# A scan of log-sum-exp on one core: an opening store of one element per DMA engine, the last waits moved inside the block, and the last tile leaving by 1, 1 and 2 rows

## The chip, the cores and the metric

One core of a Trainium2 chip runs the kernel. The metric is device time in microseconds (us), the median of several executions. Executions of one kernel mostly agree within 0.3 us of 1250. "PE" is the matrix engine, "DVE" the vector engine, "ACT" the scalar engine (it also issues the stores), "POOL" or GpSimd the general engine (it makes two masks and has little else to do), "SP" the sync engine (it issues the loads).

## The reference, cut to what matters

```python
x: (8, 4096, 2048) float32
out[:, 0] = x[:, 0]
for t in range(1, 4096):
    out[:, t] = logaddexp(out[:, t - 1], x[:, t])     # written out with max, exp and log
```

That is a running log of a sum of exponentials along the second axis: exp, a running sum, then log. 268 MB come in and 268 MB go out.

## The kernel before

The 4096 rows of each batch are cut into tiles of 512 rows (128 partitions with 4 rows each, 2048 columns). There are 64 tiles of 4 MB and six buffers of 32 KB per partition. For each tile ACT takes exp; DVE adds the 4 rows of each partition (L186); PE adds the sums of the partitions before (L166) and the carry of the tile before (L155); DVE adds both in (L195); ACT takes Ln (L130) and issues the store (L135). SP issues a load as soon as the store of the buffer's last content has landed (L110).

```python
for rows, c in ((slice(0, 2), top), (slice(2, R), loaded[0])):        # L84, before the block
    c(nc.sync.dma_start(out=ti[0][:, rows, :], in_=x_v[0][:, rows, :]), 16)
with nc.Block() as block:
    ...
    # SP
    for n in range(1, NT):
        i = n % NI
        if n >= NI:
            sp.wait_ge(stored[i].s, n // NI * 16)
        loaded[i](sp.dma_start(out=ti[i][:], in_=x_v[n]), 16)
    ...
    # ACT, tile n, half h of the columns; parts(n) is the whole tile, two halves for the last one
    for rows in parts(n) if h else [slice(0, R)]:
        logs(act.activation(t[:, rows, half[h]], t[:, rows, half[h]], ACT.Ln)._wait_ge(carried[h].s, n + 1))
        if h:
            act.wait_ge(logs.s, logs.n)
            stored[n % NI](act.dma_start(out=o_v[n][:, rows, :], in_=t[:, rows, :]), 16)
    # ACT's order: exp(0); for n: exp(n + 1), ln(n)
    ...
for c in stored:                                                       # after the block
    nc.sync.wait_ge(c.s, c.n)
```

The softmax here doesn't subtract the row's maximum and nothing guards it: scores larger than these inputs give would overflow.

## Time and profile before

| | before |
|---|---|
| time, median of the three executions known when the prediction was made | 1250.37 us (1250.36 to 1250.6) |
| span of the profiled execution | 1248.8 us |
| first load packet | 2.04 us |
| first store issued / its first packet | 38.93 / 43.55 us |
| last load lands / last store lands | 1207.88 / 1246.77 us |
| last landing to span's end | 2.06 us |

Times inside an execution are from the span's start. A *semaphore* is a counter that instructions and transfers of the kernel raise and on which its engines wait; a transfer has *landed* with the last step that it adds there. Two readings beyond the page's lines are used throughout. A *packet record* is the start and duration of one piece of a transfer on one of the 16 DMA engines (a 32 KB packet normally takes 1.213 us, a 16 KB one 0.611 us: the medians in before, where 16038 of the 16128 packets of 32 KB took under 1.23 us). *Excess* is what packets took beyond that, summed over a stretch and divided by the 16 engines: the time that each engine lost. The profile's lines of before are in the prediction below.

### The profile page before, as it was taken

The numbers are of one execution on the slowest core, as the hardware profiler recorded it, in microseconds if no ns is written. First come the engines' busy times: TensorE is split into PE (matmuls) and PEld (weight loads), VectorE is DVE, ScalarE is ACT, GpSimd is POOL, SyncE is SP. The second block draws the span as 40 slices with busy tenths as digits, with TensorE's granted clock in tenths as the row PEclk, the third lists the DMA queues.
The fourth block names the chain that finished last, engine by engine and source line by source line (L and its number), as shares of the span: only waits on it lengthen the run. The fifth ranks groups of instructions, "written<-read, shape, count | busy, mean of one in ns | idle before, by whom it ended". The sixth has DMA issues, their size and how long they took to land.

```text
span 1248.8 us, 2916 instructions
## 1 busy us (share of the span) xinstructions
PE 645.1 (52%) x960; PEld 213.4 (17%) x960; DVE 1022.3 (82%) x512; ACT 907.5 (73%) x259; POOL 1.1 (0%) x8
## 2 busy tenths in 40 slices
PE   2655456553556444655465544555545564455551
PEld 0211112111112111211111111111111121111110
DVE  5999978778787787887878878778787787877873
ACT  5987866867768677686776866867768677686773
POOL 0000000000000000000000000000000000000000
PEclk9899788787887868777678786787767878778776
DMA  9999999999999999999999999999999999999998
GB/s 403 420 431 431 430 437 436 427 434 432 437 435 426 435 432 437 433 428 435 431 437 433 430 435 430 437 431 432 436 430 436 432 432 435 431 436 432 431 435 361
DMA packets 18735, 537.06 MB, mean 430 GB/s; under 512 B 2080, under 2 KB 2080, under 8 KB 2080
## 3 DMA queue, kind: packets, MB, share of 16 engines
q1 hardware_dynamic: 9360, 268.44, 49.9%
q10 hardware_dynamic: 9360, 268.44, 49.8%
q8 instruction: 7, 0.11, 0.0%
q14 instruction: 8, 0.07, 0.0%
HBM read 268.44 MB, written 268.44 MB: 430 GB/s over the span
## 4 chain that ended last, share of the span: by engine, by line
DMA 80%; ACT 14%; DVE 4%; PE 1%; DVEq 0%; issue 0%; SPq 0%; ACTq 0%; PEldq 0%
DMA out_dram<-ti 41%; DMA ti<-in_x_dram 38%; ACT ti L130 7%; ACT ti L121 7%; DVE ti L195 2%; DVE ti L186 1%; PE ps L166 1%; DVEq L86 0%; PE ps L155 0%; SPq L84 0%; ACTq L135 0%; PEldq L151 0%; SPq L233 0%; SPq L69 0%
## 5 line engine op out<-in xcount | busy, mean ns | idle before, releaser
L121 ACT ACTIVATE ti<-ti 128x4096 f32<-128x4096 f32 (+1 forms) x128 | 452.5, 3582 | 308.2 <-DMA ti<-in_x_dram 306.0
L186 DVE TENSOR_TENSOR ti<-ti 128x1024 f32<-128x1024 f32 x384 | 464.6, 1224 | 196.6 <-ACT ti L121 187.9
L195 DVE TENSOR_TENSOR ti<-ti,ps 128x4096 f32<-128x4096 f32 x128 | 560.0, 4416 | 9.0 <-PE ps L166 8.8
L166 PE MATMUL ps<-ti,before 128*128 128x512 f32 x512 | 373.2, 879 | 347.1 <-DVE ti L186 347.0
L130 ACT ACTIVATE ti<-ti 128x4096 f32<-128x4096 f32 x129 | 455.8, 3576 | 9.5 <-PE ps L155 6.6
L155 PE MATMUL ps<-ti,last 128*128 128x512 f32 x448 | 271.9, 738 | 228.9 <-DVE ti L195 228.9
L166 PEld LDWEIGHTS ps<-ti,before 128*128 128x128 f32 x512 | 127.5, 276 | 607.4 <-DVE ti L186 503.2
L155 PEld LDWEIGHTS ps<-ti,last 128*128 128x128 f32 x448 | 85.9, 212 | 399.5 <-DVE ti L195 332.8
L119 ACT ACTIVATE ti<-ti 128x4096 f32<-128x4096 f32 x1 | 3.6, 3616 | 6.3 <-DMA ti<-in_x_dram 6.3
L30 ACT ACT_TABLE_LOAD x1 | 1.3, 1283 | 0.8 <-PEq L222 0.8
L94 POOL TENSOR_SCALAR_AFFINE_SELECT before<-before 128x128 f32<-128x128 f32 x1 | 0.3, 292 | 0.1
L99 POOL TENSOR_SCALAR_AFFINE_SELECT last<-last 128x128 f32<-128x128 f32 x1 | 0.3, 292 | 0.0
L90 POOL MEMSET before<- 128x128 f32 x1 | 0.2, 204 | 0.5 <-SPq L69 0.5
L91 POOL MEMSET last<- 128x128 f32 x1 | 0.2, 204 | 0.0
L222 POOL MEMSET const-bfloat16-1.0<- 128x1 bf16 x1 | 0.1, 101 | 0.0
L222 POOL MEMSET const-uint8-127<- 128x1 uint8 x1 | 0.1, 101 | 0.0
L222 POOL MEMSET const-float32-0.0<- 128x1 f32 x1 | 0.1, 98 | 0.3 <-issue 0.3
L222 POOL MEMSET const-float32-1.0<- 128x1 f32 x1 | 0.1, 98 | 0.0
## 6 DMA issues: line engine op xcount, KB each, us to landing
ti<-in_x_dram SPq DMA_DIRECT2D x63, 4096.0 KB, 38.5
out_dram<-ti ACTq DMA_DIRECT2D x63, 4096.0 KB, 44.0
ti<-in_x_dram SPq DMA_DIRECT2D x2, 2048.0 KB, 9.6
out_dram<-ti ACTq DMA_DIRECT2D x2, 2048.0 KB, 13.2
```

Source lines behind the costliest of these rows:

```text
L30: nc.scalar.preload_act_table_set("natural_log_exp_and_others")
L90: ones(g.memset(before[:], 1.0))
L94: shaped(g.affine_select(out=before[:], in_=before[:], compare_op=mybir.AluOpType.is_ge, fill=0.0, base=-1, pattern=[[1, P]], channel_mult ...
L99: shaped(g.affine_select(out=last[:], in_=last[:], compare_op=mybir.AluOpType.is_ge, fill=0.0, base=-(P - 1), pattern=[[0, P]], channel_mu ...
L119: act.activation(t[:, :lo], t[:, :lo], ACT.Exp)._wait_ge(top.s, 16)
L121: a = act.activation(t[:, lo:, half[h]], t[:, lo:, half[h]], ACT.Exp)
L130: logs(act.activation(t[:, rows, half[h]], t[:, rows, half[h]], ACT.Ln)._wait_ge(carried[h].s, n + 1))
L155: m = pe.matmul(ps[(n + 1) % 2][:, sl], last[:], ti[n % NI][:, R - 1, sl], start=True, stop=False, skip_group_check=True,)
L166: m = pe.matmul(ps[n % 2][:, sl], before[:], ti[n % NI][:, R - 1, sl], start=n % NBLK == 0, stop=True, skip_group_check=True,)
L186: a = dve.tensor_add(t[:, r, cols], t[:, r - 1, cols], t[:, r, cols])
L195: joined[h](dve.tensor_add(t[:, :, cols], t[:, :, cols], ps[n % 2][:, cols].unsqueeze(1).to_broadcast([P, R, HALF]),)._wait_ge(ahead[h].s, ...
L222: nc = _bacc.Bacc("TRN2", target_bir_lowering=False, num_devices=1)
```

## The change

Its intent: pay at the start, where nothing flows, what the prediction takes for the cost of the store queue's first use (0.89 us of each DMA engine at 40 us); have fewer instructions after the last store has landed; give the last rows to the DMA engines sooner. The core of the diff, cut:

```diff
-        m = 2 if n == NT - 1 else 1
-        return [slice(k * R // m, (k + 1) * R // m) for k in range(m)]
+        return [slice(0, 1), slice(1, 2), slice(2, R)] if n == NT - 1 else [slice(0, R)]
...
-            self.s, self.n = tc.alloc_semaphore(name), 0
+            self.s, self.n = nc.alloc_semaphore(name), 0
...
+        def settle(self, engine):     # one instruction: wait until the count is n, then subtract n
...
-    with tc.tile_critical():
+    with tc.tile_critical(no_gpsimd_drain=True):
...
-        with nc.Block() as block:
+        with nc.Block(no_gpsimd_drain=True) as block:
             @block.scalar
             def _(act):
+                with nc.allow_non_contiguous_dma(reason="one element per DMA engine"):
+                    warm(act.dma_start(
+                        out=o_v[0][0:16, 0, 0:1], in_=nc.const_aps.tensor(0.0, [16, 1], f32)
+                    ), 16)
...
                 exp(0)
+                warm.now(act)         # wait for the opening store
...
+            @block.sync               # the first two loads move in here
...
+                for n in range(NT - NI, NT):
+                    stored[n % NI].settle(sp)
...
+            @block.gpsimd             # at its end, once ACT, PE and DVE have said they are over
+                over.now(g)
+                for c in every:
+                    if c not in stored:
+                        c.settle(g)
-        for c in stored:
-            nc.sync.wait_ge(c.s, c.n)
```

More of the change, by code (lines that the diff above doesn't have):

```diff
@@ L53, in parts @@
     def parts(n):
-        m = 2 if n == NT - 1 else 1
-        return [slice(k * R // m, (k + 1) * R // m) for k in range(m)]
+        return [slice(0, 1), slice(1, 2), slice(2, R)] if n == NT - 1 else [slice(0, R)]
+    every = []
     class Count:
         def __init__(self, name):
-            self.s, self.n = tc.alloc_semaphore(name), 0
+            self.s, self.n = nc.alloc_semaphore(name), 0
+            every.append(self)
         def __call__(self, inst, by=1):
@@ L66, in __call__, with add, now @@
             self.n += by
-            return self.n
-    with tc.tile_critical():
+        def add(self, engine):
+            engine.sem_inc(self.s, 1)
+            self.n += 1
+        def now(self, engine):
+            engine.wait_ge(self.s, self.n)
+        def settle(self, engine):
+            if self.n:
+                engine.add_instruction(mybir.InstEventSemaphore(
+                    name=f"I-{nc.next_id()}", engine=engine.engine, ins=[], outs=[],
+                    sync_info=mybir.SyncInfo(
+                        on_wait=[mybir.SyncWait(
+                            sync_type="semaphore", id=self.s.num, ant_name=self.s.name,
+                            wait_mode="sem-ge-imm", wait_value=self.n,
+                        )],
+                        on_update=[mybir.SyncUpdate(
+                            sync_type="semaphore", id=self.s.num, ant_name=self.s.name,
+                            update_mode="sem-sub-imm", update_value=self.n,
+                        )],
+                    ),
+                ))
+    with tc.tile_critical(no_gpsimd_drain=True):
         def counts(name, n):
             return [Count(f"{name}{i}") for i in range(n)]
-        ones, shaped, logs, top, chain = (
-            Count(s) for s in ("ones", "shaped", "logs", "top", "chain")
+        ones, shaped, logs, top, chain, warm, over = (
+            Count(s) for s in ("ones", "shaped", "logs", "top", "chain", "warm", "over")
         )
@@ L80 @@
         )
-        for rows, c in ((slice(0, 2), top), (slice(2, R), loaded[0])):
-            c(nc.sync.dma_start(out=ti[0][:, rows, :], in_=x_v[0][:, rows, :]), 16)
-        with nc.Block() as block:
-            @block.gpsimd
-            def _(g):
-                ones(g.memset(before[:], 1.0))
-                ones(g.memset(last[:], 1.0))
-                g.wait_ge(ones.s, ones.n)
-                shaped(g.affine_select(
-                    out=before[:], in_=before[:], compare_op=mybir.AluOpType.is_ge, fill=0.0,
-                    base=-1, pattern=[[1, P]], channel_multiplier=-1,
-                ))
-                shaped(g.affine_select(
-                    out=last[:], in_=last[:], compare_op=mybir.AluOpType.is_ge, fill=0.0,
-                    base=-(P - 1), pattern=[[0, P]], channel_multiplier=1,
-                ))
-            @block.sync
-            def _(sp):
-                for n in range(1, NT):
-                    i = n % NI
-                    if n >= NI:
-                        sp.wait_ge(stored[i].s, n // NI * 16)
-                    loaded[i](sp.dma_start(out=ti[i][:], in_=x_v[n]), 16)
+        with nc.Block(no_gpsimd_drain=True) as block:
             @block.scalar
             def _(act):
+                with nc.allow_non_contiguous_dma(reason="one element per DMA engine"):
+                    warm(act.dma_start(
+                        out=o_v[0][0:16, 0, 0:1], in_=nc.const_aps.tensor(0.0, [16, 1], f32)
+                    ), 16)
                 def exp(n):
@@ L133, in ln @@
                             if h:
-                                act.wait_ge(logs.s, logs.n)
+                                logs.now(act)
                                 stored[n % NI](act.dma_start(
@@ L143, in _ @@
                     ln(n)
+                over.add(act)
+            @block.sync
+            def _(sp):
+                for rows, c in ((slice(0, 2), top), (slice(2, R), loaded[0])):
+                    c(sp.dma_start(out=ti[0][:, rows, :], in_=x_v[0][:, rows, :]), 16)
+                for n in range(1, NT):
+                    i = n % NI
+                    if n >= NI:
+                        sp.wait_ge(stored[i].s, n // NI * 16)
+                    loaded[i](sp.dma_start(out=ti[i][:], in_=x_v[n]), 16)
+                for n in range(NT - NI, NT):
+                    stored[n % NI].settle(sp)
             @block.tensor
@@ L150, in carry @@
                         pe.wait_ge(joined[h].s, n + 1)
-                        pe.sem_inc(carried[h].s, 1)
+                        carried[h].add(pe)
                         return
@@ L172, in triangle @@
                     ahead[h](m)
-                pe.wait_ge(shaped.s, shaped.n)
+                pe.wait_ge(shaped.s, 2)
                 for n in range(NT):
@@ L179, in _ @@
                         carry(n, h)
+                over.add(pe)
             @block.vector
@@ L204, in _ @@
                         join(n, h)
-        for c in stored:
-            nc.sync.wait_ge(c.s, c.n)
+                over.add(dve)
+            @block.gpsimd
+            def _(g):
+                ones(g.memset(before[:], 1.0))
+                ones(g.memset(last[:], 1.0))
+                ones.now(g)
+                shaped(g.affine_select(
+                    out=before[:], in_=before[:], compare_op=mybir.AluOpType.is_ge, fill=0.0,
+                    base=-1, pattern=[[1, P]], channel_multiplier=-1,
+                ))
+                shaped(g.affine_select(
+                    out=last[:], in_=last[:], compare_op=mybir.AluOpType.is_ge, fill=0.0,
+                    base=-(P - 1), pattern=[[0, P]], channel_multiplier=1,
+                ))
+                over.now(g)
+                for c in every:
+                    if c not in stored:
+                        c.settle(g)
 _INS = ['x']
```

## The prediction

Its sum came to -0.7 + 0.1 + 0.0 = -0.6 us on 1250.37, so 1249.8, and 1249.7 with the lean. The 0.2 us at the head, which is in the -0.7, is an estimate: that the first issues of ACT and SP hold each other up was not shown. The "fetches" are the transfers that the page of before lists as q8 and q14, kind "instruction": 7 of 16 KB and 8 of 8 KB. "1.213 us everywhere else" is the normal time: 27 other 32 KB packets of before took 1.30 us or more, 14 of them started within 1 us after a fetch did. "No such excess" at later stores is at most 0.09 us in the 7 us after an issue.

> **What bounds the kernel now.** I read the page's slices first, then its queues, the stretches, the sync engine's waits and the timeline of the two ends.
>
> The slices (40 equal slices of the span; the digit is the busy share in tenths) and the queues:
>
> ```profile
> span 1248.8 us, 2916 instructions
> DMA  9999999999999999999999999999999999999998
> ...
> q1 hardware_dynamic: 9360, 268.44, 49.9%
> q10 hardware_dynamic: 9360, 268.44, 49.8%
> ```
>
> The transfers are busy in every slice; loads (q1) and stores (q10) share the 16 DMA engines almost evenly. 536.9 MB must move whatever the change does. The stretches (columns: busy time of PE, PEld, DVE, ACT, POOL, then PE clock, DMA share, GB/s) show where the rate is not the usual one:
>
> ```profile
> 20.00:38.00 18.00, 13.25 (x20) 4.34 (x18) 17.58 (x11) 13.35 (x4) 0.00 (x0) 0.91 1.00 431
> 38.00:46.00 8.00, 3.97 (x8) 1.35 (x8) 8.00 (x3) 7.55 (x3) 0.00 (x0) 1.00 0.95 360
> 46.00:60.00 14.00, 9.15 (x13) 3.08 (x14) 13.65 (x9) 13.18 (x5) 0.00 (x0) 0.76 1.03 447
> 100.00:1200.00 1100.00, 582.79 (x861) 192.76 (x860) 914.39 (x460) 805.93 (x229) 0.00 (x0) 0.78 1.00 433
> ```
>
> The middle runs at 433 GB/s with the DMA share at 1.00: no kernel change to a few instructions can touch it. Only one stretch after the start is slow, 38 to 46 us (a part of its bytes is booked in the next: over the 22 us from 38 to 60 the mean is (8 x 360 + 14 x 447) / 22 = 415 GB/s, which is 22 x (1 - 415/433) = 0.9 us short). It begins where the first store is issued:
>
> ```profile
> 38.93 0.37 ACTq L135 DMA_DIRECT2D out_dram<-ti  x1
> ```
>
> The trace's packet records say what happens there. A 32 KB packet takes 1.213 us everywhere else, but two load packets in a row on each of the 16 engines (starting between 40.28 and 42.36 us) take 1.33 to 2.06 us. Summed and divided by 16, the excess is 0.89 us per engine. The first store's own first packet only starts at 43.55 us, 4.6 us after its issue. Later stores show no such excess. So the store queue's first use costs 0.89 us of every DMA engine. (The load queue's first packets, from 2.04 us on, show 0.64 us of the same kind, over 0.611 us for 16 KB.)
>
> At the other end, the last stores and the wait for them:
>
> ```profile
> 1229.98 0.34 ACTq L135 DMA_DIRECT2D out_dram<-ti  x1
> 1230.37 1.91 ACT L130 ACTIVATE ti<-ti 128x2048 f32<-128x2048 f32 x1 [0.42 <-ACT ti L130]
> 1232.31 0.34 ACTq L135 DMA_DIRECT2D out_dram<-ti  x1
> ...
> 1222.00:1242.00 20.00, 0.00 (x0) 0.00 (x0) 5.92 (x2) 7.47 (x4) 0.00 (x0) 0.61 0.98 424
> 1242.00:1244.00 2.00, 0.00 (x0) 0.00 (x0) 0.00 (x0) 0.00 (x0) 0.00 (x0) 0.50 0.78 336
> 1244.00:1246.00 2.00, 0.00 (x0) 0.00 (x0) 0.00 (x0) 0.00 (x0) 0.00 (x0) 0.50 0.23 98
> ...
> SPq L86 <- PEq L86: 63.2, 1, 63.2
> SPq L207 <- DMA out_dram<-ti: 13.8, 1, 13.8
> ```
>
> The DMA engines stay full until 1242 us (share 0.98; in the packet records all 16 work without a gap), 10 us after the last issue: the tail is queue, not compute. They then finish unevenly: the last packets of the 16 engines end between 1242.96 and 1246.30 us, and the last semaphore step lands at 1246.77. The sync engine has passed the block's barrier (L86) long before; it waits 13.8 us for the stores alone (L207). From landing to the span's end it is 2.06 us of semaphore work.
>
> [...] The trace has fifteen such fetches after the start (8 KB in 0.31 us or 16 KB in about 0.93 us), and the spread between the first and last landing of a transfer's 16 steps grows from 0.5 us to 3.4 us in jumps beside them (0.60 to 1.60 at 103 to 120 us, 1.93 to 2.65 at 703 to 720, 2.68 to 3.48 at 1025). [...]
>
> **The change, part by part.**
>
> *Opening store.* ACT issues 16 elements before anything else. It should pay the store queue's first use at about 1 to 3 us, beside the load queue's own first use, and while no stream is running yet. Removed at 40 us: 0.89 us on each engine, on the path (share 1.00), so the end moves by all of it. Added at the head: ACT and SP leave the opening barrier together (branches at 0.841 and 0.863 us)[...]. The sync engine's first issue took 0.376 us. [...] Part of the first-use cost may still fall on loads. I take 0.2 us. Net: -0.7 us. The wait for it stands after the first exponentials (over 15 us), so is met already.
>
> *Last tile as 1, 1 and 2 rows.* A half-width Ln over 4 rows takes 3.62 us, over 2 rows 1.91 us: 1.71 us for 2048 elements, so about 1.05 us for one row. From 1228.04: end of first piece 1229.1, second about 1230.6, third about 1232.9. The first issue comes 0.85 us sooner, the last 0.6 us later. Does either matter? With 9.7 us of each engine's last 4 MB store to do, the quickest engine (ending 1242.96) reaches the last tile at about 1233.2 and its second half at 1238.1. Both old issues (1229.98 and 1232.31) and both new ones are well before. So nothing is gained. 16 KB packets take 0.611 and 32 KB 1.213 us, so a packet costs about 9 ns beside its bytes; 8 more packets per engine add 0.07 us. Net: +0.1 us.
>
> *Waits inside the block.* Before, four waiting instructions on SP run one after the other from 1246.788 to 1246.981; in the changed order the store that lands last is waited for last, and only that one instruction stands after it: -0.2 us. But the block's barrier now comes after the landing. The closing barrier of the same trace takes 0.244 us from SP's drain (1247.992) to its next instruction (1248.236), and one more drain stands ahead: +0.3 us. GpSimd's drain is dropped on the way out. Its record is short (41 ns), but SP stands still from 1247.396 to 1247.803 before the instruction that waits for GpSimd's count. If that hole is the drain's, 0.4 us go; the count is recorded as raised at 1247.221, so I give it one chance in three: -0.13 us. The 23 counts that GpSimd takes back, at some 0.07 us each (as SP's waits above), start when ACT is done at about 1233.3 and last 1.6 us, hidden under the stores. Net: 0.0 us.
>
> *Sum.* -0.7 + 0.1 + 0.0 = -0.6 us, on 1250.37: 1249.8. I lean a little lower, to 1249.7, as the first use might overlap fully.
>
> **The rivals.**
>
> *The first-use cost only moves.* The engines pay 0.89 us at 2 us instead of 40 us, in front of the load stream. For it: loads suffered at 40 us though the stores were the new ones. Against: at 1 us no data flows. It would give 1250.4 to 1250.6.
>
> *The drain is the hole at the end, and the first use vanishes.* Then -0.9 - 0.4 + 0.2: about 1249.2.
>
> *Uneven engines decide.* The end is the slowest engine's, 1.5 us behind the next group (1246.30 against 1244.86). If added instructions shift or add a fetch on it, the end moves by some 0.8 us either way (the jumps above). [...]
>
> *The tail is starved.* If ACT's pieces fed the engines just in time, finer pieces would gain about 0.85 us. The share until 1242 us, and no gap in the packet records, speak against it.
>
> **Range and chances.** The two larger rivals put 1249.2 and 1250.6 as natural ends; a moved fetch widens it. Range 1248.8 to 1250.6. 2% is 25 us; nothing in either end is that big, since the head up to the first load packet is 2.0 us and the tail after the last landing 2.1 us. Chances: faster 0.01, same 0.98, slower 0.01.
>
> **What would show it.** Right: no packets of 1.3 to 2.1 us around 40 us, the stretch 38 to 46 us back near 433 GB/s; the first load packet at 2.0 to 2.3 us; last tile's issues at 0.85 us sooner to 0.6 us later relative to the Ln start, with the share full till the end; landing to span's end within 1.8 to 2.3 us. Wrong: long load packets at 2 to 5 us that add up to 1.5 us (the cost moved); the hole before SP's last but one wait gone; a landing spread at the end other than 3.4 us (fetches moved).

## The result, and the profile after

| | before | after |
|---|---|---|
| time, median of six | 1250.51 us (1250.36 to 1250.6) | 1250.68 us (1250.5 to 1250.79) |
| span of the profiled execution | 1248.8 us | 1249.0 us |
| excess at the first full store | 0.89 us | 0.99 us |
| last landing to span's end | 2.06 us | 1.97 us |

The ratio is 1.0001 (95% interval 0.9988 to 1.0014): the same. A ratio is the mean time of one kernel's fast runs over that of the other's of the same rounds, so it is not quite the ratio of the medians quoted. 1250.68 lies 0.08 us above the predicted range and 1 us above the predicted time.

The stretches after (time, busy time of PE, PEld, DVE, ACT, POOL, then PE clock, DMA share, GB/s) that answer to those of before:

```profile
20.00:38.00 18.00, 10.87 (x20) 3.56 (x18) 17.58 (x11) 14.60 (x5) 0.00 (x0) 1.00 0.99 430
38.00:46.00 8.00, 4.77 (x8) 1.61 (x8) 8.00 (x3) 6.78 (x2) 0.00 (x0) 0.86 0.96 360
46.00:60.00 14.00, 7.24 (x15) 2.52 (x15) 13.86 (x9) 13.07 (x4) 0.00 (x0) 0.96 1.03 447
100.00:1200.00 1100.00, 595.41 (x860) 195.97 (x858) 914.33 (x459) 804.28 (x228) 0.00 (x0) 0.77 1.00 433
...
1222.00:1242.00 20.00, 0.80 (x2) 0.00 (x0) 7.21 (x2) 8.96 (x5) 0.00 (x0) 0.66 0.98 418
```

The last column is the reading: 360 and then 447, to the digit what the kernel before had. The slow stretch at the first full store is still there. The first full store was issued at 37.25 us, and 30 load packets that start between 39.1 and 42.7 us take 1.25 to 2.17 us; before it was 32 packets of 1.33 to 2.06. The opening store did run, as the timeline (start, duration, issuer, line) and the page's DMA issues (last column: us from issue to landing) show:

```profile
0.99 0.42 ACTq L115 DMA_DIRECT2D out_dram<-const-float32-0.0  x1
...
1.02 0.85 SPq L156 DMA_DIRECT2D ti<-in_x_dram  x2
...
out_dram<-const-float32-0.0 ACTq DMA_DIRECT2D x1, 0.1 KB, 3.6
```

Its 16 elements are 16 packets of 4 B that start at 3.27 to 3.67 us, each 5 to 6 ns ahead of one of 16 load packets that then run at the same time: one on each engine. They landed at 4.3 to 4.6 us, and the opening store did not delay the loads: their first packet starts at 2.02 us (2.04 before). It simply bought nothing (0.99 us of excess at the first full store, 0.89 before). The last tile and the waits (timeline, then SP's own waits):

```profile
1229.33 1.06 ACT L135 ACTIVATE ti<-ti 128x1024 f32<-128x1024 f32 x1 [0.71 <-PEq L72]
1230.42 0.34 ACTq L140 DMA_DIRECT2D out_dram<-ti  x1
1230.80 1.06 ACT L135 ACTIVATE ti<-ti 128x1024 f32<-128x1024 f32 x1 [0.41 <-ACT ti L135]
1231.89 0.34 ACTq L140 DMA_DIRECT2D out_dram<-ti  x1
1232.27 1.91 ACT L135 ACTIVATE ti<-ti 128x2048 f32<-128x2048 f32 x1 [0.41 <-ACT ti L135]
1234.21 0.34 ACTq L140 DMA_DIRECT2D out_dram<-ti  x1
...
SPq L82 <- SPq L82: 78.7, 6, 19.4
```

Counted from the start of the last tile's second Ln, the issues stand at 1.09, 2.56 and 4.88 us, against 1.94 and 4.27 before. The DMA engines have about ten more microseconds of work at that point: the last issue ends at 1234.55 us, and their share is still 0.96 from 1242 to 1244 us. SP now takes the six counts back as its stores land (six waits), so one such instruction is left for the last landing.

### The profile page after: what moved, and what is told of

It reads as the page before. It is cut to its first block, busy times and chain, and to the rows that moved or that the text cites. A ratio compares the mean times of both kernels' runs of the same rounds, so it can differ in the third digit from the quotient of the medians.

```text
span 1249.0 us, 2951 instructions
## 1 busy us (share of the span) xinstructions
PE 656.9 (53%) x960; PEld 216.1 (17%) x960; DVE 1023.6 (82%) x512; ACT 907.7 (73%) x260; POOL 1.1 (0%) x8
## 4 chain that ended last, share of the span: by engine, by line
DMA 80%; ACT 14%; DVE 4%; PE 1%; DVEq 1%; issue 0%; ACTq 0%; SPq 0%; PEldq 0%
DMA ti<-in_x_dram 41%; DMA out_dram<-ti 39%; ACT ti L135 7%; ACT ti L126 7%; DVE ti L216 2%; DVE ti L207 2%; PE ps L186 1%; DVEq L109 1%; PE ps L175 0%; ACTq L140 0%; SPq L156 0%; PEldq L72 0%; SPq L273 0%; SPq L96 0%
## 5 line engine op out<-in xcount | busy, mean ns | idle before, releaser
L126 ACT ACTIVATE ti<-ti 128x4096 f32<-128x4096 f32 (+1 forms) x128 | 452.5, 3582 | 309.1 <-DMA ti<-in_x_dram 307.5
L186 PE MATMUL ps<-ti,before 128*128 128x512 f32 x512 | 381.5, 897 | 331.3 <-DVE ti L207 330.7
L135 ACT ACTIVATE ti<-ti 128x4096 f32<-128x4096 f32 (+1 forms) x130 | 455.9, 3550 | 10.3 <-PE ps L175 7.0
L175 PE MATMUL ps<-ti,last 128*128 128x512 f32 x448 | 275.5, 747 | 234.6 <-DVE ti L216 234.6
L124 ACT ACTIVATE ti<-ti 128x4096 f32<-128x4096 f32 x1 | 3.6, 3616 | 6.2 <-DMA ti<-in_x_dram 6.2
```

What stands on the lines that cost most here:

```text
L124: act.activation(t[:, :lo], t[:, :lo], ACT.Exp)._wait_ge(top.s, 16)
L126: a = act.activation(t[:, lo:, half[h]], t[:, lo:, half[h]], ACT.Exp)
L175: m = pe.matmul(ps[(n + 1) % 2][:, sl], last[:], ti[n % NI][:, R - 1, sl], start=True, stop=False, skip_group_check=True,)
L186: m = pe.matmul(ps[n % 2][:, sl], before[:], ti[n % NI][:, R - 1, sl], start=n % NBLK == 0, stop=True, skip_group_check=True,)
```

## The experiments

"Excess" is that at the first full store, read from the packet records within 7 us of its issue. "Before" is the kernel before on the same chip in the same rounds.

| run | median us (range) | before | first full store issued | excess there | landing to end |
|---|---|---|---|---|---|
| e1 without the opening store | 1250.47 (1250.38 to 1250.57) | 1250.47 | 37.88 | 0.97 | 1.97 |
| e2 opening store alone | 1250.41 (1250.18 to 1252.06) | 1250.47 | 37.85 | 0.80 | 2.05 |
| e3 waits alone | 1250.42 (1250.31 to 1250.9) | 1250.47 | 38.92 | 0.83 | 1.96 |
| e4 pieces alone | 1250.71 (1250.65 to 1251.1) | 1250.47 | 38.25 | 0.84 | 2.06 |
| e5 opening 128 x 512 B | 1254.15 (1250.78 to 1279.85) | 1250.68 | 37.45 | 0.82 | 2.05 |
| e6 opening 32 KB, 16 neighbours, at 23 us | 1253.7 (1253.56 to 1253.97) | 1250.68 | 47.84 | 0.00 | 2.06 |
| e7 store queue dry mid-run | 1251.71, one execution | 1250.68 | 38.15 | 0.98 | 2.06 |
| e8 fewer DVE instructions | 1272.66 (1272.07 to 1272.98) | 1250.68 | 42.99 | 0.91 | 1.95 |
| e9 opening 32 KB memory to memory | 1251.75 (1251.67 to 1251.8) | 1250.54 | 39.11 | 0.95 | 1.97 |
| e10 opening 8 KB out of a buffer | 1250.89 (1250.78 to 1251.51) | 1250.54 | 38.20 | 0.91 | 1.95 |
| e11 change without the pieces | 1250.65 (1250.41 to 1250.85) | 1250.54 | 37.36 | 0.90 | 1.96 |
| e12 opening 32 KB out of a buffer | 1265.1 (1251.48 to 1270.33) | 1250.55 | 38.88 | 0.02 | 1.97 |
| e13 first store late, no opening | 1250.56, one execution | 1250.55 | 46.78 | 0.89 | 2.06 |
| e14 first store later still | 1252.91, one execution | 1250.55 | 56.61 | 0.62 | 2.06 |
| e15 opening 16 KB out of a buffer | 1254.2 (1251.04 to 1259.66) | 1250.6 | 38.76 | 0.84 | 1.95 |
| e16 e12 once more | 1251.66 (1251.47 to 1258.5) | 1250.6 | 39.14 | 0.01 | 1.97 |

In e5, e12, e15 and e16 some executions were 4 to 29 us longer than the shortest of the same kernel, while those of before in the same rounds were within about 2 us of each other. In e12's slow profile the loads lose 10.9 us per engine and the stores 0.8, nearly all from 312 us on, far from the change. Why is open. It happened only in kernels with an opening store out of on-chip memory (e2, e6, e10, e11 and the changed kernel have one too and did not show it); whether the opening store causes it is not shown, and nothing is concluded from those times.

### First set: the parts one by one

e1 removes the opening store from the changed kernel; e2 puts it alone into the kernel before; e3 has the waits inside the block, without opening store and with two halves; e4 has the pieces alone. The edits are the parts of the diff above.

> The changed kernel without its opening store. Theory A (the opening store does nothing: the cost at the first big store is not a first use of the queue): the first big store's load packets are again 0.9 to 1.0 us per engine too long, and the time is that of the changed kernel within 0.15 us (1250.5 to 1250.8). Theory B (the opening store gains its 0.9 us, but another part of the change loses as much): the time rises by 0.6 to 0.9 us over the changed kernel, to 1251.3 or more.

> The kernel before with the opening store alone. Theory A: the excess of the load packets at the first big store stays at 0.8 to 1.0 us per engine and the time is that of the kernel before within 0.15 us (1250.35 to 1250.65). Theory B: excess under 0.2 us and 1249.6 to 1249.8.

> The kernel before with its last waits inside the block and the counts taken back there, without opening store and with the two halves. From the two traces (2.06 us from last landing to span's end before, 1.97 us after) this part alone should gain 0.1 us: 1250.3 to 1250.5, with landing to end at 1.95 to 2.0 us. The rival, that the barrier after the landing costs as much as it first seems (+0.3 us), would show 2.2 us or more.

> The kernel before with the last tile leaving by 1, 1 and 2 rows. If the finer pieces only add packets (8 more of 9 ns per engine, and one more landing), the time rises by 0.1 us, to 1250.5 to 1250.7. If they fed an engine that ran dry, it would fall by up to 0.8 us. If the gaps in the packet records at 1224 us of the changed kernel come from them, gaps show here too; if they come from the order of loads and stores that happens to arise at the first store, they need not.

Measured: the excess stays at 0.80 to 0.97 us with the opening store (e2) and without it (e1, e3, e4), and neither e1 nor e2 moves the time by more than 0.06 us from the kernel before. Theory A stands and theory B falls: the opening store does not gain something that another part loses again. (e1's time lies 0.03 us under the range given for theory A.) e3 shortens the way from landing to end to 1.96 us as expected, 0.1 us, which its median (0.05 us lower) is too coarse to confirm. e4 costs 0.24 us in the medians; the packets alone account for 0.1. Its own DMA engines had no gap at the tail.

### Second set: what is used for the first time?

e5 and e6 try opening stores with more in them; e7 asks whether the cost comes back when the store queue starts again; e8 goes after another loss at the end, the uneven finish of the engines.

```diff
 e5 (kernel before with an opening store; wait for it after exp(0) as in the change)
+    act.wait_ge(shaped.s, 2)
+    warm(act.dma_start(out=o_v[0][:, 0, 0:P], in_=before[:]), 16)
 e6 (after exp(0))
+    act.wait_ge(loaded[1].s, 16)
+    warm(act.dma_start(out=o_v[1][0:16], in_=ti[1][0:16]), 16)
+    act.wait_ge(warm.s, warm.n)
 e7 (in ln, before the store)
+    if n == 20:
+        act.wait_ge(loaded[24 % NI].s, (24 // NI + 1) * 16)
 e8 (in DVE's loop; one wait for the second half's exp)
-    a = dve.tensor_add(t[:, r, cols], t[:, r - 1, cols], t[:, r, cols])    # twice three a tile
+    a = dve.tensor_add(t[:, r, :], t[:, r - 1, :], t[:, r, :])             # three a tile
```

> The kernel before with another opening store: 128 rows of 512 bytes, eight packets on each DMA engine, at about 2 us. Theory C (the cost at the first big store is a first use that one packet of 4 bytes per engine is too little to pay[...]): the excess at the first big store falls from 0.8 to 1.0 us per engine to under 0.3. Theory D (it is paid whenever a stream of big stores starts beside loads[...]): it stays at 0.8 to 1.0.

> The kernel before with an opening store of one full packet of 32 KB per engine (the raw rows of 16 partitions of tile 1, written again later), issued when tile 1 has landed, at about 23 us, and waited for. Theory C: long load packets at 23 to 28 us, and none (under 0.3 us per engine) at the first full store after it. Theory D: long load packets at both, 0.5 to 1.0 us each, so the time rises by up to 1 us. If the excess needs several packets per engine, only the first full store shows it, with 0.8 to 1.0.

> The kernel before, but the store of tile 20 is held until load 24 has landed, so that the store queue runs dry for some 10 us in the middle of the run while loads go on, and then starts again beside load 25. Theory C or any first use: no long load packets at the restart (excess under 0.2 us per engine). Theory D: 0.6 to 1.0 us per engine of long load packets at the restart, as at the first store. The time itself rises by several us, because loads wait for the held store; that is on purpose.

> The kernel before with the waits inside the block, and with the vector engine's six half-width sums of a tile as three of full width: 5 instead of 8 instructions a tile[...]. If the uneven end of the DMA engines (last landings spread over 3.4 us) comes from fetches that all fall on one engine, the spread falls by some 1.6 us and the end with it by 0.5 to 1.5 us, to 1249.0 to 1250.0. If the spread has another source, or another engine is then the last, the time stays within 0.2 us of 1250.4.

e5: 128 packets of 512 B instead of 16 of 4 B change nothing (0.82 us). e6: no long load packets at its first full store, for the first time. But its opening packets took 2.8 to 3.9 us each, so that the time is 3 us longer. The load packets beside them show only 0.02 us of excess in the 7 us after that issue, which neither theory expected. e7 at its restart (stretches):

```profile
432.00:446.00 14.00, 0.00 (x0) 0.00 (x0) 0.00 (x0) 3.23 (x1) 0.00 (x0) 0.50 1.02 440
446.00:454.00 8.00, 3.79 (x5) 1.31 (x6) 7.26 (x6) 8.00 (x4) 0.00 (x0) 0.50 0.98 422
454.00:470.00 16.00, 9.85 (x16) 3.10 (x16) 15.83 (x8) 15.59 (x5) 0.00 (x0) 0.82 1.01 433
```

No store packet runs from 432.3 to 445.9 us; then the store issued at 442.38 starts. Its neighbours among the load packets show 0.00 us of excess in the 7 us after the issue, and the rate stays at 422 or above. So the cost is not that of any start of a store stream beside loads: theory D falls for stores, and a cost that stores pay once is left. (For loads see e14 below. In e7 itself the load issued at 461.71 us, after 7.5 us without load packets, shows 0.10 us beside it, and the next store 0.20.)

e8 is a miss, and it did not test what it was made for. (The 1.6 us in its expectation was the author's estimate; it rested on a count of fetches that was not shown.) The waits before (first line) and in e8 (second), as waiter, releaser, us in total, times, longest:

```profile
DVE ti L195 <- PE ps L166: 8.8, 40, 0.2
```

```profile
DVE ti L213 <- PE ps L183: 239.7, 64, 3.9
```

With full-width sums DVE can no longer work on one half while PE handles the other: it waits for PE once in each of the 64 tiles, 3.7 us on average (239.7 / 64). From 600 to 1100 us the rate is still 433 GB/s, as before. The rate in its last stretches, where before had 429 (1210 to 1230), shows the DMA engines starved:

```profile
1210.00:1230.00 20.00, 11.21 (x18) 3.63 (x16) 16.47 (x6) 14.12 (x5) 0.00 (x0) 0.83 0.54 233
1230.00:1250.00 20.00, 10.74 (x16) 3.73 (x16) 16.06 (x6) 8.07 (x3) 0.00 (x0) 0.74 0.55 236
```

The run shows how little room compute has at the end of this kernel: its last load lands at 1203.63 us, 4 us sooner than before, and then the stores wait for compute; the kernel ends 22 us later. Whether fetches make the end uneven stays argued, not shown; e8's trace has 14 of them after the start, before's 15.

### Third set: memory to memory, a small packet out of a buffer, and the pieces

```diff
 e9 (change with two halves; opening store replaced)
+    warm(act.dma_start(out=o_v[0][0:16], in_=x_v[0][0:16]), 16)
 e10 (the same; DVE fills the rows first, and SP's load of buffer 5 waits for the store)
+    filled(dve.memset(ti[5][:, 0, :], 0.0))
+    act.wait_ge(filled.s, 1)
+    warm(act.dma_start(out=o_v[0][0:P:8, 0, :], in_=ti[5][0:P:8, 0, :]), 16)
 e11: the changed kernel with two halves
```

> The changed kernel with two halves and another opening store: 16 rows of 32 KB copied from the input to the output, so a full-size packet on each engine that reads no on-chip memory, issued at 1.0 us. If what is used for the first time is a large write to the output (theory C1), the long load packets at the first full store go (under 0.3 us per engine, against 0.8 to 1.0 so far) and the time is 1250.0 to 1250.9 (the copy's own 1.2 us per engine stand against the gain). If it is the reading of on-chip memory by large packets (C2), they stay at 0.8 to 1.0 and the time is 1251.3 to 1251.8.

> The changed kernel with two halves and an opening store of one 8 KB packet per engine, from 16 partitions eight apart of a buffer that the vector engine has just filled, at 2 to 4 us. Under C1 and C2 both, if 8 KB are enough, the long load packets at the first full store go (under 0.3 us per engine) and the time is 1249.6 to 1250.2, with part of the cost moved to 3 to 6 us. If a first use needs more than 8 KB, or cannot be moved, they stay at 0.8 to 1.0 and the time is 1250.5 to 1251.0.

> The changed kernel with the last tile in two halves again (opening store and waits inside the block kept). If the pieces cost what e4 says (0.1 us of packets, 0.24 us in the medians), the time is 1250.35 to 1250.55, 0.1 to 0.3 us below the changed kernel. If the pieces gained anything against a tail that ran dry, it is 1250.8 or more.

e9: a full 32 KB packet on each engine into the output, read from memory. It ran beside loads at 5.8 to 8.0 us, took its normal 1.213 us with no excess beside it, and the first full store still cost 0.95 us. The time, 1251.75, is the kernel before plus the packet's 1.2 us: as C2 expected. So a first use of the queue, a first full-size packet and a first large write to the output, made this early, do not pay the cost. e10: 8 KB out of a buffer are not enough either (0.91 us). e11 misses its number by 0.1 us, 1250.65 against 1250.54 for before on that chip; the pieces' cost of e4 does not show here. What the pieces cost in time is therefore not settled beyond 0.1 us of packets.

### Fourth set: the control, and a full packet out of a buffer

```diff
 e12 (as e10, with all 32 KB of the 16 partitions filled and stored)
+    filled(dve.memset(ti[5][:], 0.0))
+    warm(act.dma_start(out=o_v[0][0:P:8], in_=ti[5][0:P:8]), 16)
 e13 and e14 (kernel before; after exp(0), k = 2 in e13, k = 3 in e14)
+    act.wait_ge(loaded[k].s, 16)
```

> As the 8 KB opening store, but the whole 32 KB of each of 16 partitions eight apart, one full packet per engine out of on-chip memory, at about 10 us. If large reads of on-chip memory by a store are what has to have happened once (C2), the long load packets at the first full store go (under 0.3 us per engine) and turn up beside the opening store, or not at all; the time is 1250.5 to 1251.9, as the packet itself costs 1.2 us. If not, they stay at 0.8 to 1.0 there and the time is 1251.4 to 1252.2.

> The kernel before, with the second tile's exponentials held until load 2 has landed, so that the first full store is issued at 47 to 48 us as in the run with the 32 KB opening store at 23 us, but without any opening store. If that run lost its long packets to its opening store, they are here at 0.8 to 1.0 us per engine. If they depend on how many loads are still queued at the first store (theory E), they are under 0.3 here too.

> The same, held until load 3 has landed: the first full store is issued at 57 us, when only some 5 us of loads are left in the queue. Theory E: no long packets (under 0.2 us per engine). A first use of stores: 0.8 to 1.0 us per engine as ever, if load packets are left to show it.

e13 is the control for e6: its first store comes at 46.78 us, e6's at 47.84, and without an opening store the cost is there in full (0.89 us). Its stretches:

```profile
46.00:54.00 8.00, 3.37 (x8) 1.35 (x8) 7.97 (x4) 7.55 (x3) 0.00 (x0) 1.00 1.02 393
54.00:68.00 14.00, 7.80 (x14) 2.19 (x12) 13.90 (x7) 13.58 (x5) 0.00 (x0) 0.89 0.99 428
```

Over these 22 us the mean is (8 x 393 + 14 x 428) / 22 = 415 GB/s, the same as over the 22 us from 38 to 60 before. The dip has moved with the store. e14 shows 0.62 us with only 5 us of loads left, so theory E falls. e14 also shows that such a cost can come back. Its load queue was empty from 63.19 us; the next load was issued at 72.10 and its first packet started at 77.47. In between, 32 *store* packets (two per engine) that start from 73.26 to 75.90 us take 1.26 to 2.32 us: 0.80 us per engine, the size and shape of the cost at the first store, with loads and stores in each other's place. After the store issued at 85.76, 16 load packets show another 0.40 us. No run was made to find out when it comes back, so "once" holds here for stores that start again, not for every queue. e12 has 0.02 us at its first full store, and 0.66 us beside its opening store.

### Fifth set: the clean repeat, and half the size

e16 is e12's kernel again. e15 is the same with 16 KB of each partition.

> As the 8 KB and 32 KB opening stores out of on-chip memory, with 16 KB on each of 16 partitions eight apart, at about 6 us. If 16 KB are enough to have the cost paid early, the long load packets at the first full store are under 0.3 us per engine, some 0.6 us of them stand beside the opening store instead, and the time is 1250.6 to 1251.0 (0.6 us for the packet itself, nothing gained). If not, they stay at 0.8 to 1.0 and the time is 1251.0 to 1251.3.

> The run with one 32 KB packet per engine from 16 partitions eight apart once more, because three of its four executions were slow and its profile fell in one of these. In a fast profile: under 0.1 us per engine of long load packets at the first full store, 0.5 to 0.7 us beside the opening store at 10 to 16 us; time 1251.3 to 1251.6, 1.2 us for the packet itself less what is saved. If the slow executions belong to this kernel, most are again above 1255.

The stretches of e16, whose profile is of a fast execution:

```profile
8.00:16.00 8.00, 0.00 (x0) 0.00 (x0) 1.86 (x2) 5.64 (x3) 0.00 (x0) 1.00 1.06 426
...
38.00:46.00 8.00, 5.61 (x10) 1.56 (x8) 7.74 (x4) 7.57 (x3) 0.00 (x0) 0.88 1.02 438
46.00:60.00 14.00, 5.98 (x13) 2.07 (x13) 13.86 (x9) 13.40 (x5) 0.00 (x0) 1.00 0.98 424
```

The first full store, issued at 39.14 us, now passes at 438 and 424 GB/s: (8 x 438 + 14 x 424) / 22 = 429 where before had 415, and 0.01 us of excess. Part of the cost is beside the opening store instead: 0.59 us per engine within 7 us of its issue at 9.71, against 0.89. The opening packet itself takes 1.21 us. So the estimate of the balance from these three is 1.21 + 0.59 - 0.89 = +0.9 us; the three executions of 1251.47 to 1251.79 have a median of 1251.54, 0.9 us above before's 1250.6. The fourth, 1258.5, is the only one above 1255, so the slow ones were not the rule here as they had been in e12. e15: 16 KB are not enough, 0.84 us remain at the first full store and 0.17 stand beside the opening one.

So the cost at the first full store goes when an earlier store has moved full 32 KB packets out of on-chip memory (e6, e12, e16). It was not taken apart from the time of the issue: the openings that paid were issued at 9.7 and 23.2 us, all others at 1.0 to 5.4 us; in e10, e15 and e12 the issue moves with the size, because DVE takes longer to fill more of the buffer (in e16 ACT stands idle for 8.28 us until DVE's fill is done). A small opening store issued late, or a full one out of on-chip memory issued early, was not run, so the rule "more than 16 KB" is argued and not shown. An opening of this kind costs more engine time (1.21 us for the packet and 0.59 beside it) than there is to save (0.89 us). No variant that ran beats the kernel before: the best medians, e2's 1250.41 and e3's 1250.42, are within 0.06 us of it. *Why* a first large store lengthens load packets is not shown by any run. One fact for whoever looks further: in before all 32 long load packets start (40.27 to 42.36 us) ahead of the store's own first packet (43.55), and in e16 all 16 do (12.58 to 13.03, against 14.30). So no packet of the store was on record yet when they started.

## Why the prediction was wrong

Point by point, by the prediction's own steps:

- **What bounds the kernel: right.** 433 GB/s in the middle before and after; in e9 an added 1.2 us of packets per engine shows up in the end in full (1251.75 against 1250.54).
- **Opening store: this step failed.** The prediction read "the store queue's first use costs 0.89 us of every DMA engine" off the long packets at 40 us, and concluded that a first use with 16 elements would remove it. The reading of the loss was right, its name was wrong. It was seen at one first event, which was at once the queue's first use, the first write to the output, the first large packet of a store and the first large read of on-chip memory by one. In the changed kernel the store queue was first used at 0.994 us, and the first full store still cost 0.99 us per engine. Nothing was removed. Openings of 512 B, 8 KB, 16 KB, and of 32 KB from memory (e5, e10, e15, e9) removed nothing either; only e6, e12 and e16, with 32 KB out of on-chip memory and a later issue, did. This term stood in the sum as -0.7 us (-0.9 and +0.2 at the head), -0.8 with the lean to 1249.7; it measured 0. That is nearly all of the miss of 1 us. The rest lies mostly in the base, taken as 1250.37 where six executions have a median of 1250.51.
- **The cost at the head, +0.2 us: not there.** ACT did issue first (0.994 us, SP at 1.023), and the first load packet came at 2.02 us. The rival in which the cost "only moves" to the head came nearest in its number (1250.4 to 1250.6) but not in its reason: the excess in the first 8 us is 0.69 us after and 0.64 before.
- **Pieces, +0.1 us: right as to the packets.** The issues came 0.85 us sooner and 0.61 us later relative to the Ln, as worked out; the packets of both queues take 0.10 us more per engine at their usual durations. In the packet records of before the tail had no gap (0.00 us); after it, up to five engines at a time pause at 1223.6 to 1224.3 us, before the last tile's store: 0.15 us per engine. Such gaps stand in e2 (0.24), e5, e9, e10, e11, e15 and e16 too, which have no pieces, and not in e4 (0.01), which has them. They go with a last load that lands later: its last packet ends at 1208.7 or later in all the runs named as having them (1208.81 after) and at 1208.2 or sooner in before, e3 and e4. They are not of the pieces.
- **Waits inside the block, 0.0 us: -0.09 measured, by other terms.** The way from SP's wait for the last landing to the step after the barrier takes 0.372 us (1247.035 to 1247.407), against 0.342 us for the four waits before (1246.788 to 1247.130): the two sizes predicted against each other nearly cancel, +0.03 us where +0.1 was predicted. The rival that GpSimd's drain (a DRAIN instruction of 41 ns in the trace of before) is the hole falls: a hole of 0.42 us still stands on SP (1247.424 to 1247.848) with that drain gone. The gain is one that was not seen: the closing clear (EVENT_SEMAPHORE_RANGE_CLEAR on POOL) takes 0.071 us after (1248.619 to 1248.690) and 0.222 before (1248.311 to 1248.533), so -0.15; the other steps together take 0.06 us more. Why it is shorter was not shown; the estimate, from the kernels and the semaphore numbers in the two traces, is that it covers 6 counts instead of 33, as the others are taken back early.
- **Uneven engines: a rival that stayed small.** The spread of the last 16 landings is 2.79 us after and 3.47 before, but their mean is 0.27 us later (1244.94 against 1244.67), and the last lands 0.25 us later. Worked out from the packet records: +0.10 at the first store, +0.05 at the head, +0.10 for the pieces, +0.15 for the gaps at the tail, -0.10 for other long packets, together +0.3 us. Less 0.09 us after the landing, that is the 0.16 us by which the profiled spans differ (1248.83 and 1248.98). The difference in the medians, 0.17 us, is the same size, but parts of 0.1 us are at the edge of what repeated executions can tell. That 1250.68 lies so near the range's end, 1250.6, is no sign that the sum was nearly right: before itself reached 1250.6.

The range was also drawn too tight: its upper end, 1250.6, allowed for "no gain" but not for no gain and 0.1 us of added packets.

## What to carry to other kernels

A cost at the first event of a kind has as many possible causes as the event has novelties; before one builds an opening that "pays it early", the same opening should be tried in sizes and from sources that differ in one novelty each. The look that decides is not the time, which moved by at most 0.11 us in e1, e2, e3, e11 and e13, but the packets at the place where the cost was. And where the DMA engines are full from end to end, an opening transfer must cost less engine time than it saves: here 1.8 us (1.21 and 0.59) against 0.89. Sizes should be varied at the same time of issue; here they were not.
